# Adding the causal mask on VectorE instead of TensorE, and holding the head norms' small products behind a turning

## The chip, the core and the metric

The kernel runs on one core of a Trainium2 chip. A core has a matrix engine (TensorE, "PE" in the profile, with its weight loads on a row of their own, "PEld"), three engines for elementwise work (VectorE or "DVE", ScalarE or "ACT", GpSimd or "POOL"), and a queue engine (SyncE or "SP"). They run side by side and wait for each other by semaphores. TensorE writes its products to PSUM, eight banks of 128 x 512 float32; VectorE and ScalarE read them there, and all other data lie in SBUF. The metric is the device time of one execution, in microseconds (us).

## What is computed

A decoder trunk of two layers over 512 tokens of width 1024. Layer 0 mixes with attention, layer 1 with a gated short convolution, and each layer ends with a gated MLP. The change touches the attention of layer 0 alone. It has 16 heads of 64 columns: 8 softmax heads with forget gates ("fox") and 8 stick-breaking heads. Queries and keys of every head are normalised first.

```python
q_fox = rms_norm(q[:, :H_FOX], fox_q_g)
k_fox = rms_norm(k[:, :H_FOX], fox_k_g)
...
logits = einsum('bhqd,bhkd->bhqk', qi, k) * scale
logits = logits + fi[..., :, None] - cum_f[:, :, None, :]
causal = key_pos[None, :] <= q_pos[:, None]
logits = jnp.where(causal, logits, -jnp.inf)
p = jax.nn.softmax(logits, axis=-1)
...
# stick-breaking heads
w = jnp.where(strict, jnp.exp(log_beta + later), 0.0)
```

All of it is float32. Queries are handled in blocks of 128; block b sees keys 0 to (b + 1) x 128. Inside the last of these key blocks, the diagonal one, the mask is a triangle.

## The kernel before

**Precision by halves.** A float32 product is made of three products of rounded operands: each operand is split into a high half (`hi`, a rounded copy by ScalarE) and a low half (`lo`, the difference, by VectorE), and hi x hi, hi x lo and lo x hi are summed in PSUM.

**Heads in pairs, blocks in units.** Heads are taken two at a time: pairs p = 0 to 3 are softmax, 4 to 7 are stick-breaking. The query blocks of a pair form three units, `UNITS = (0, 1), (2,), (3,)`: unit 0 holds blocks 0 and 1, units 1 and 2 one block each. So there are 24 units, and the main loop goes through them by number g.

**The steps of a pair.** `queries_keys(p)` (L588) projects keys and queries, 8 steps of three products each (L313 to L315), squares them, and ends with three small groups on TensorE:
- `sums` (L601): sums of squares, 16 narrow products (L607) into a bank "c"; ScalarE copies them (L610);
- `turned_sums` (L613): two transposes (L615) into the same bank, after which VectorE computes the reciprocal roots by a chain of short operations (L617, L399 to L411) and widens them (L633);
- `rows` (L636): four or eight transposes (L640) that spread the roots over a bank "c"; VectorE multiplies (L642), and the result is split into halves (L415 on ScalarE, L416 on VectorE). Softmax pairs spread queries and keys, stick-breaking pairs the keys only.

`logits(p, u)` (L666) makes the scores of one unit: three groups of products of halves (L688), and for softmax heads a fourth with the gate sums. In front of them it calls `need`, which runs fillers until the pair's `rows` have been issued. For softmax heads, 4 products in unit 0 and 2 in the others then add the triangle to the diagonal blocks (L697): an identity in bfloat16 times a 128 x 128 mask of 0 and -1e30. VectorE takes the maximum (L705), ScalarE the exponential with its sum (L706), VectorE the reciprocal and the scaling (L708, L711). For stick-breaking heads ScalarE takes sigmoids (L726, L727), and VectorE scans and multiplies (L729, L732).

`turn(p, b, w)` (L737) transposes the weights of a block for the product with the values: into a bank "c" (L748 for blocks 0 and 1, L760 for 2 and 3, one bank for each of the two heads there), from which ScalarE takes the high half (L754, L763) and VectorE the low half (L755, L764). `weigh(p)` (L767) then multiplies with the values (L784).

**Banks.** PSUM has two banks "a", four "b" (projections and scores) and two "c" (all the small products named above, and the turned weights).

**What sets the order.** The kernel is written as one Python program that keeps a counter of TensorE time, `clock`. `spend(us)` adds an estimate to it, `after(us, fn)` puts a step on a list of due times, and a `spend` that passes a due time runs the step on the spot. `fill(us)` draws "fillers" (steps of the projections, of the values, and of the output projection of the first eight heads) until as much has been spent. In the main loop each g issues the scores of unit g, fills 1.5 (`FILL1`), weighs a pair that is complete, and turns the blocks of unit g - 1, with 3.3 (`FILL2`) of fillers behind each unit's turning. `sums` comes 3.0 after the end of a projection (`SUMS`), `turned_sums` 1.5 after `sums`, `rows` 8.0 after `turned_sums` (`ROWS`). A step of a projection spends 0.65, of the values 0.33, `sums` 0.6, `turned_sums` 0.25, `weigh` 2.4, a turning 0.22 a key block. From the order thus written, a scheduler of the framework sets each engine's queue; it keeps to it except where it expects that an instruction is not ready, and then takes later ones first. On the chip each engine runs its own queue in order.

Of the kernel before, what the change touches and what calls it, by code (L numbers as in the profile page):

```python
# [25 lines left out]
P = 128  # L26
S = 512
NB = S // P
# [14 lines left out]
NORM0 = 4.6  # L43
ORDER = (1, 0, 1, 1, 1, 1, 3)
SUMS, FLAT, ROWS = 3.0, 1.5, 8.0
NSUMS, NROWS, LATE = 4.0, 3.0, 7.0
FILL1, FILL2, BEFORE = 1.5, 3.3, 2.0
UNITS = (0, 1), (2,), (3,)
# [7 lines left out]
def trunk(  # L56
# [167 lines left out]
    def flush():  # L224
        while later:
            later.pop(0)[2]()

    def fill(us):
        quota[0] += us
# [358 lines left out]
    def queries_keys(p):  # L588


        fox = p < 4
        v = tiny.tile([P, 2, NB, 2], F32, tag="qv", name=f"qv{p}")
        r = tiny.tile([P, 2, NB, 2], F32, tag="qr", name=f"qr{p}")
        kept, got, sqs = {}, {}, []
        halves[p] = got

        def pair(i):
            got[i] = [aw.tile([P, S], F32R, tag=f"qk_{n}{i}", name=f"qk_{n}{p}{i}", bufs=2) for n in ("hi", "lo")]
            return got[i]

        def sums():  # L601


            t = bank("c")
            for i in range(2):
                for b in range(NB):
                    pe.matmul(t[32 * b:32 * (b + 1), i * P:(i + 1) * P], head_ones, sqs[i][:, b * P:(b + 1) * P], start=True, stop=True)  # L607
            spend(0.6)
            flat = own.tile([P, S], F32, tag="nrow", name=f"flat{p}", bufs=1)[:, 0:2 * P]
            act.activation(flat, t[:, 0:2 * P], AF.Copy)  # L610
            after(FLAT, lambda: turned_sums(t, flat))

        def turned_sums(t, flat):  # L613
            for i in range(2):
                pe.transpose(t[:, (2 + i) * P:(3 + i) * P], flat[:, i * P:(i + 1) * P], ident)  # L615
            spend(0.25)
            dve.scalar_tensor_tensor(  # L617
                v.rearrange("p i b h -> p (i b) h"), t[:, 2 * P:4 * P].rearrange("p (j c) -> p j c", c=32)[:, :, 0:2],
                1.0 / HD, least[:, :, None].to_broadcast([P, 2 * NB, 2]), op0=ALU.mult, op1=ALU.add,
            )  # L620
            scales()

        def scales():
            vf, rf = (t.rearrange("p i b h -> p (i b h)") for t in (v, r))
            rsqrt(rf, vf, 16, f"qk{p}")
            if not fox:
                s = q_scale[p] = aw.tile([P, 2, NB, 2], F32, tag="qscale", name=f"qscale{p}", bufs=3)
                dve.tensor_copy(s[:, 0], r[:, 1])
                dve.tensor_scalar(s[:, 1], r[:, 1], -1.0, None, op0=ALU.mult)
            wides = {}  # L630
            for i in kept:
                wides[i] = work.tile([P, S], F32, tag="u0", name=f"qwide{p}{i}").rearrange("p (b h d) -> p b h d", b=NB, h=2)
                dve.tensor_copy(wides[i], r[:, i][:, :, :, None].to_broadcast([P, NB, 2, HD]))  # L633
            after(ROWS, lambda: rows(wides))

        def rows(wides):  # L636
            for i in kept:
                t = bank("c")
                for b in range(NB):
                    pe.transpose(t[:, b * P:(b + 1) * P], wides[i][:, b].rearrange("p h d -> p (h d)"), ident)  # L640
                n = work.tile([P, S], F32, tag="y", name=f"qn{p}{i}")
                dve.tensor_tensor(n, kept[i], t, op=ALU.mult)  # L642
                split(*pair(i), n)
            done.add(("qk", p))

        for i in range(2):
            acc = bank("b" if p >= 1 else "a")
            yield from products(acc, weights())
            sq = own.tile([P, S], F32, tag="sq", name=f"sq_{p}{i}")
            act.activation(sq, acc, AF.Square)  # L650
            g = head_gains[:, (0 if fox else 2) + (1 - i):][:, 0:1]
            if i == 1 and not fox:
                hi, lo = pair(i)
                act.activation(hi, acc, AF.Copy, scale=g)
                dve.scalar_tensor_tensor(lo, acc, g, f32(hi), op0=ALU.mult, op1=ALU.subtract)
            else:
                kept[i] = work.tile([P, S], F32, tag="u1", name=f"qk{p}{i}", bufs=3)
                act.activation(kept[i], acc, AF.Copy, scale=g)
            sqs.append(sq)
        after(SUMS, sums)  # L660

    def at_once(u):

# [2 lines left out]
    def logits(p, u):  # L666


        fox = p < 4
        need(("qk", p))  # L670
        need("decay")
        (k_hi, k_lo), (q_hi, q_lo) = (halves[p][i] for i in range(2))
        bs = UNITS[u]
        ss = [bank("b") for _ in range(2)]

        parts, at_ = [], 0
        for i, b in enumerate(bs):
            n = (b + 1) * P
            parts.append((b, n, 256 * i, at_))
            at_ += n  # L680
            spend((4 if fox else 3) * max(n, 256) * 0.00044 + (0.12 if fox else 0))

        def scores(ql, kl, first, last):
            for b, n, c, _ in parts:
                wide = max(n, 256)
                for e in range(2):
                    rows = slice(e * HD, (e + 1) * HD)
                    pe.matmul(ss[e][:, c:c + wide], ql[rows, b * P:n], kl[rows, 0:wide], start=first and b == bs[0], stop=last and b == bs[-1])  # L688

        scores(q_hi, k_hi, True, False)  # L690
        scores(q_hi, k_lo, False, False)
        scores(q_lo, k_hi, False, not fox)
        if fox:
            scores(dl[:, p, :], dr, False, False)
            for e in range(2):
                for b, n, c, _ in parts:
                    pe.matmul(ss[e][:, c + b * P:c + n], ident16, mask, start=False, stop=b == bs[-1])  # L697
        w = aw.tile([P, 2, S], F32, tag="w", name=f"w{p}{u}", bufs=2)
        own = [w[:, :, a:a + n] for b, n, c, a in parts]
        if fox:  # L700
            m = len(bs)
            top, total, inv = (tiny.tile([P, m, 2], F32, tag=f"{t}{m}", name=f"{t}{p}{u}") for t in ("top", "total", "inv"))
            for j, (b, n, c, a) in enumerate(parts):
                for e in range(2):
                    dve.reduce_max(top[:, j, e:e + 1], ss[e][:, c:c + n], axis=AX.X, negate=True)  # L705
                    act.activation(own[j][:, e, :], ss[e][:, c:c + n], AF.Exp, bias=top[:, j, e:e + 1], accum_out=total[:, j, e:e + 1])  # L706
            for es in at_once(u):
                dve.reciprocal(inv[:, :, es], total[:, :, es])  # L708
                for j in range(m):
                    for e in range(es.start, es.stop):  # L710
                        dve.tensor_scalar(own[j][:, e, :], own[j][:, e, :], inv[:, j, e:e + 1], None, op0=ALU.mult)  # L711
        else:

            scale = q_scale[p]
            if not rests:
                rests.append(aw.tile([P, 2, S + 1], F32, tag="rest", name="rest", bufs=1))
                dve.memset(rests[0][:, :, S:S + 1], 0.0)
            rest = rests[0]
            if u == 0:
                dve.memset(rest[:, :, P:P + 1], 0.0)  # L720
            for es in at_once(u):
                for j, (b, n, c, a) in enumerate(parts):
                    end = P if b == 0 else S
                    keys = slice(end - n, end)
                    for e in range(es.start, es.stop):
                        act.activation(rest[:, e, keys], ss[e][:, c:c + n], AF.Sigmoid, scale=scale[:, 1, b, e:e + 1])  # L726
                        act.activation(own[j][:, e, :], ss[e][:, c:c + n], AF.Sigmoid, scale=scale[:, 0, b, e:e + 1])  # L727
                        back = rest[:, e, keys][:, ::-1]
                        dve.tensor_tensor_scan(back, back, begin[:, S - n:S][:, ::-1], 0.0, op0=ALU.mult, op1=ALU.max)  # L729
                for j, (b, n, c, a) in enumerate(parts):  # L730
                    end = P if b == 0 else S
                    dve.tensor_tensor(own[j][:, es], own[j][:, es], rest[:, es, end - n + 1:end + 1], op=ALU.mult)  # L732
        return [(b, x) for (b, n, c, a), x in zip(parts, own)]
# [3 lines left out]
    def turn(p, b, w):  # L737
# [18 lines left out]
        else:  # L756
            for e in range(2):
# [4 lines left out]
                hi, lo = (t_[:, to:to + b + 1, :].rearrange("p k q -> p (k q)") for t_ in pts[p])  # L762
                act.activation(hi, t[:, 0:n], AF.Copy)  # L763
                dve.tensor_tensor(lo, t[:, 0:n], f32(hi), op=ALU.subtract)  # L764
        spend(0.22 * (b + 1))

    def weigh(p):  # L767
# [922 lines left out]
```

## Time and profile before

| | us |
|---|---|
| median of 3 runs (1127.93 to 1128.21) | 1127.98 |
| the profiled execution | 1127.62 |
| its span | 1125.3 |
| TensorE busy | 1115.6 |
| VectorE busy | 943.4 |
| ScalarE busy | 679.9 |

How the lines in the next part are read. A row of a timeline has the start and the length in us, the engine, the line of the kernel, the operation, `out<-in` by the program's names, the shape, a count (like neighbours are merged) and, in brackets, how long the engine was idle before it and what ended that. `psa`, `psb` and `psc` are the banks. A row of the view of waits has the waiting engine and line, whom it waited for, the sum in us, the count and the longest. A row of busy time by stretch has the stretch, its length, and the busy time and count of PE, PEld, DVE, ACT and POOL, then the granted clock of TensorE, the share of the DMA engines and GB/s. A row of a group has the count, the busy time in all and the mean length of one in ns, then the idle time before them and what ended it. TensorE's products overlap, so the length of one is longer than the step from one start to the next.

### The profile page before, as it was taken

How to read it: one execution, taken by the hardware profiler on the slowest of the kernel's cores; microseconds unless marked ns; L12 is line 12 of the kernel's file. 1: busy time of each engine (PE TensorE's matmuls, PEld its weight loads, DVE VectorE, ACT ScalarE, POOL GpSimd, SP SyncE). 2: the span in 40 equal slices, each digit the busy share in tenths (PEclk: the TensorE clock that was granted, in tenths of full speed). 3: DMA queues.
4: the chain of work that ended last, by engine and by line, in shares of the span. 5: the costliest groups of instructions: out<-in, count | busy, mean ns of one | idle time of the engine just before them, and what ended most of it. 6: DMA issues, size and time to landing. Idle time of an engine off the chain costs nothing.

```text
span 1125.3 us, 19407 instructions
## 1 busy us (share of the span) xinstructions
PE 1115.6 (99%) x7691; PEld 1009.8 (90%) x7691; DVE 943.4 (84%) x1439; ACT 679.9 (60%) x1013; POOL 158.6 (14%) x191
## 2 busy tenths in 40 slices
PE   9999999999999999999999999999999999999998
PEld 7888787878899999999999899988889999998886
DVE  6787888887899787888989889875799888898886
ACT  7556676655466766666557455543456766677553
POOL 4011111111101110014400001111111110014300
PEclk9999999999999999999999999999999999999999
DMA  6678777687877777799963455798887766699951
GB/s 194 173 180 200 179 180 200 155 205 206 197 208 201 208 192 197 206 277 205 228 173 77 120 153 125 157 229 216 207 208 188 177 174 159 183 265 195 233 153 57
DMA packets 175690, 209.34 MB, mean 186 GB/s; under 512 B 7564, under 2 KB 140220, under 8 KB 175600
## 3 DMA queue, kind: packets, MB, share of 16 engines
q0 software_dynamic: 41024, 86.95, 39.1%
q1 hardware_dynamic: 134416, 121.09, 34.8%
q8 instruction: 60, 0.98, 0.4%
q14 instruction: 30, 0.25, 0.1%
q10 hardware_dynamic: 160, 0.07, 0.0%
HBM read 203.10 MB, written 49.28 MB: 224 GB/s over the span
## 4 chain that ended last, share of the span: by engine, by line
PE 90%; DVE 4%; issue 2%; DMA 2%; ACT 1%; SPq 0%; DVEq 0%; ACTq 0%; POOLq 0%
PE psb L1056 25%; PE psb L1602 11%; PE psa L1056 10%; PE psa L1602 8%; PE psb L313 5%; PE psb L315 5%; PE psb L314 5%; PE psa L315 3%; PE psa L313 3%; PE psa L314 3%; PE psa L784 2%; PE psb L688 2%; DMA Xc<-in_conv_w_in 2%; PE psb L570 1%; PE psc L315 1%
## 5 line engine op out<-in xcount | busy, mean ns | idle before, releaser
L292 ACT ACTIVATE whi<-raw 128x1024 fp32r<-128x1024 f32 (+2 forms) x89 | 91.7, 1031 | 93.6 <-PE psb L314 29.9
L293 DVE TENSOR_TENSOR wlo<-raw,whi 128x1024 fp32r<-128x1024 f32 (+2 forms) x89 | 105.5, 1185 | 24.2 <-ACT whi L292 23.2
L1056 PE MATMUL psb<-p_lo,whi_p 128*128 128x256 f32 x432 | 121.7, 282 | 0.0
L1056 PE MATMUL psb<-p_hi,wlo_p 128*128 128x256 f32 x432 | 121.6, 281 | 0.0
L1056 PE MATMUL psb<-p_hi,whi_p 128*128 128x256 f32 x432 | 121.4, 281 | 0.0
L313 PE MATMUL psb<-hs_a,whi 128*128 128x512 f32 x224 | 92.2, 412 | 0.0
L315 PE MATMUL psb<-hs_a,wlo 128*128 128x512 f32 x224 | 88.7, 396 | 0.0
L1056 PEld LDWEIGHTS psb<-p_hi,whi_p 128*128 128x128 f32 x432 | 81.9, 190 | 0.0
L1056 PEld LDWEIGHTS psb<-p_lo,whi_p 128*128 128x128 f32 x432 | 81.4, 188 | 0.0
L1056 PE MATMUL psa<-p_hi,wlo_p 128*128 128x256 f32 x288 | 81.2, 282 | 0.0
L1056 PEld LDWEIGHTS psb<-p_hi,wlo_p 128*128 128x128 f32 x432 | 81.2, 188 | 0.0
L1056 PE MATMUL psb<-q_lo,whi_q 128*128 128x256 f32 x288 | 81.1, 282 | 0.0
L1056 PE MATMUL psa<-p_lo,whi_p 128*128 128x256 f32 x288 | 81.1, 282 | 0.0
L1056 PE MATMUL psb<-q_hi,wlo_q 128*128 128x256 f32 x288 | 81.1, 281 | 0.0
L1056 PE MATMUL psa<-p_hi,whi_p 128*128 128x256 f32 x288 | 80.9, 281 | 0.0
L1056 PE MATMUL psb<-q_hi,whi_q 128*128 128x256 f32 x288 | 80.9, 281 | 0.0
L1602 PE MATMUL psb<-act,whi 128*128 128x256 f32 x352 | 63.2, 282 | 0.0
L423 DVE SCALAR_TENSOR_TENSOR uv<-yv,taps,uv 128x511 f32<-128x511 f32 (+1 forms) x80 | 56.6, 744 | 0.0
L1602 PE MATMUL psb<-whi,act 128*128 128x512 f32 x176 | 56.4, 398 | 0.0
L423 DVE SCALAR_TENSOR_TENSOR ug<-yg,taps,ug 128x511 f32<-128x511 f32 (+1 forms) x80 | 55.5, 744 | 0.0
L1056 PEld LDWEIGHTS psa<-p_hi,whi_p 128*128 128x128 f32 x288 | 54.5, 189 | 0.1
L1056 PEld LDWEIGHTS psb<-q_hi,whi_q 128*128 128x128 f32 x288 | 54.6, 189 | 0.0
(478 smaller groups left out, 3619.3 us busy)
## 6 DMA issues: line engine op xcount, KB each, us to landing
t<-in_ffn_w_up POOLq DMA_DIRECT2D x42, 768.0 KB, 8.0
t<-t POOLq DMA_DIRECT2D x18, 768.0 KB, 5.5
raw<-in_attn_w_in SPq DMA_DIRECT2D x24, 512.0 KB, 5.3
X<-in_ffn_w_up SPq DMA_DIRECT2D x18, 512.0 KB, 5.1
Y<-t SPq DMA_DIRECT2D x18, 512.0 KB, 6.6
three<-t SPq DMA_DIRECT2D x18, 512.0 KB, 3.7
W<-in_ffn_w_up SPq DMA_DIRECT2D x18, 512.0 KB, 4.0
X<-in_ffn_w_up POOLq DMA_DIRECT2D x18, 512.0 KB, 8.0
```

The lines of the kernel that those rows point to most:

```text
L292: return (act.activation(hi[:, at_], raw[:, at_], AF.Copy), dve.tensor_tensor(lo[:, at_], raw[:, at_], f32(hi[:, at_]), op=ALU.subtract))
L293: dve.tensor_tensor(lo[:, at_], raw[:, at_], f32(hi[:, at_]), op=ALU.subtract))
L313: made = [pe.matmul(acc, w[0], rhs[0], start=first, stop=False), pe.matmul(acc, w[0], rhs[1], start=False, stop=False), pe.matmul(acc, w[1 ...
L314: pe.matmul(acc, w[0], rhs[1], start=False, stop=False),
L315: pe.matmul(acc, w[1], rhs[0], start=False, stop=last)]
L423: dve.scalar_tensor_tensor(dst[:, d:], src[:, 0:S - d], tap(j), dst[:, d:], op0=ALU.mult, op1=ALU.add)
L570: pe.matmul(acc, lhs[0], w[0], start=first, stop=False)
L688: pe.matmul(ss[e][:, c:c + wide], ql[rows, b * P:n], kl[rows, 0:wide], start=first and b == bs[0], stop=last and b == bs[-1])
L784: pe.matmul(out_, w, t[:, first:first + step * (NB - k - 1) + 1:step, :], start=k == 0 and i == 0, stop=k == NB - 1 and i == 1)
L1056: pe.matmul(to, w[a][:, k, c], x[b][:, k, :], start=fresh and i + k + t == 0, stop=i == 1 and k == 3 and t == 2, skip_group_check=not fresh)
L1602: pe.matmul(to, l, r, start=begin and o + t == 0, stop=end and t == 2 and o == (0 if layer else 1), skip_group_check=not fresh)
```

## The change

1. In `logits`, the mask products of the softmax heads go. The fourth group of scores now ends the accumulation. Instead, before the first maximum of each head of a unit, VectorE adds the mask in place in PSUM, to all diagonal blocks of that head's bank at once: two blocks (columns 0 to 127 and 384 to 511) in unit 0, one in units 1 and 2. The estimate that `logits` spends for a softmax unit keeps its 0.12 a block for the mask.
2. `turn` notes the counter's value at its end and whether the pair is a stick-breaking one. A new function `clear` delays a step until the counter is 2.3 (softmax) or 4.5 (stick-breaking) past that, and looks again then. `sums` and `rows`, when they come due, go through it; `turned_sums` doesn't.

```diff
+CLEAR = 2.3, 4.5
...
+    turned = [-1e9, 0]
+
+    def clear(fn):
+
+        wait = turned[0] + CLEAR[turned[1]] - clock[0]
+        if wait > 0:
+            after(wait, lambda: clear(fn))
+        else:
+            fn()
...
-            after(ROWS, lambda: rows(wides))
+            after(ROWS, lambda: clear(lambda: rows(wides)))
...
-        after(SUMS, sums)
+        after(SUMS, lambda: clear(sums))
...
         if fox:
-            scores(dl[:, p, :], dr, False, False)
-            for e in range(2):
-                for b, n, c, _ in parts:
-                    pe.matmul(ss[e][:, c + b * P:c + n], ident16, mask, start=False, stop=b == bs[-1])
+            scores(dl[:, p, :], dr, False, True)
...
                 for e in range(2):
+                    if j == 0:
+                        diag = ss[e].rearrange("p (k q) -> p k q", q=P)[:, bs[0]:NB:3, :]
+                        dve.tensor_tensor(diag, diag, mask[:, None, :].to_broadcast([P, m, P]), op=ALU.add)
                     dve.reduce_max(top[:, j, e:e + 1], ss[e][:, c:c + n], axis=AX.X, negate=True)
...
+        turned[:] = clock[0] + 0.22 * (b + 1), p >= 4
         spend(0.22 * (b + 1))
```

## The prediction

> **What bounds the kernel now.** I read the page first, then busy time by stretch, then who waited for whom on TensorE, then the timelines around those waits.
>
> ```profile
> span 1125.3 us, 19407 instructions
> PE 1115.6 (99%) x7691; PEld 1009.8 (90%) x7691; DVE 943.4 (84%) x1439; ACT 679.9 (60%) x1013; POOL 158.6 (14%) x191
> ...
> PE 90%; DVE 4%; issue 2%; DMA 2%; ACT 1%; SPq 0%; DVEq 0%; ACTq 0%; POOLq 0%
> ```
>
> TensorE is busy for 99% of the span and holds 90% of the chain that ended last. So an instruction taken from TensorE is worth its own issue time, and a wait of TensorE is worth its length, wherever they lie. The profiled execution took 1127.62 us, 2.3 over its span; the median of the runs is 1127.98, 0.36 more. The sum is made against 1127.62.
>
> The change touches the attention stage only: softmax heads, about 48 to 148 us, then stick-breaking heads to 258 us.
>
> ```profile
> 48.00:148.00 100.00, 99.40 (x711) 81.11 (x709) 80.29 (x213) 62.35 (x141) 12.61 (x17) 1.00 0.77 184
> 148.00:258.00 110.00, 107.41 (x696) 88.50 (x689) 95.13 (x184) 71.11 (x139) 13.24 (x18) 1.00 0.76 189
> ```
>
> The third busy figure is VectorE: 80% in the first stretch, 86% in the second. It has time left in both, but it is a queue that runs in order, so what counts is how late it is when TensorE wants something back.
>
> ```profile
> PE psc L640 <- DVE pt L764: 1.3, 1, 1.3
> PE psc L607 <- DVE pt L764: 1.1, 2, 0.7
> PE psa L784 <- DVE o L791: 0.5, 1, 0.5
> PE psa L784 <- DVE h L830: 0.2, 1, 0.2
> ```
>
> These are all the waits of TensorE from 48 to 258 us that the view names. The two largest rows are the second half of the change: L607 (sums of squares of a head pair) and L640 (its spreading) want one of the two banks "c" that `turn` filled, and VectorE has not yet taken the low half of the turned weights out (L764). The three places are:
>
> ```profile
> 128.51 0.64 PE L607 MATMUL psc<-sq,head_ones 128*32 128x128 f32 x16 [0.44 <-DVE pt L764]
> ...
> 196.38 0.66 PE L640 MATMUL psc<-ident,qwide 128*128 128x128 f32 x4 [1.32 <-DVE pt L764]
> ...
> 205.10 0.65 PE L607 MATMUL psc<-sq,head_ones 128*32 128x128 f32 x16 [0.66 <-DVE pt L764]
> ```
>
> They are the sums of pair 4, the rows of pair 6 and the sums of pair 7: 0.44 + 1.32 + 0.66 = 2.42 us, the first two rows of the waits.
>
> **The mask, TensorE's side.** Per softmax pair 4 + 2 + 2 small products go, 32 in all. The stick-breaking heads run the same scores without a mask, so the trace shows both forms. From the last group of scores to the second product behind it:
>
> ```profile
> 97.44 0.40 PE L688 MATMUL psb<-dr,dl 64*128 64x256 f32 x4
> 97.77 0.40 PE L697 MATMUL psb<-mask,begin 128*128 128x128 bf16 x4
> ...
> 98.29 0.40 PE L314 MATMUL psb<-hs_a,whi 128*128 128x512 f32 x1
> ...
> 104.52 0.33 PE L688 MATMUL psb<-dr,dl 64*128 64x384 f32 x2
> ...
> 105.19 0.39 PE L314 MATMUL psb<-hs_a,whi 128*128 128x512 f32 x1
> ```
>
> ```profile
> 172.80 0.40 PE L688 MATMUL psb<-qk_hi,qk_lo 64*128 64x256 f32 x4
> ...
> 173.47 0.40 PE L314 MATMUL psb<-hs_a,whi 128*128 128x512 f32 x1
> ...
> 179.53 0.34 PE L688 MATMUL psb<-qk_hi,qk_lo 64*128 64x384 f32 x2
> ...
> 180.13 0.39 PE L314 MATMUL psb<-hs_a,whi 128*128 128x512 f32 x1
> ```
>
> With four masks 98.29 - 97.44 = 0.85, without 173.47 - 172.80 = 0.67: 0.18 gained. With two masks 105.19 - 104.52 = 0.67, without 0.60: 0.07. Per pair 0.18 + 0.07 + 0.07 = 0.32, over four pairs **-1.3 us**. The 0.40 us that the view shows for four masks is pipeline depth and would overstate it. The Trainium skill (TensorE: Matmul & The Clock Gate, Back-to-back issue gap) gives about 81 ns for each 128-column product in a stream; by it the 32 would be worth an estimated 2.6 us and the forecast would lie 1.3 lower. The rows go against that: four of them cost 0.18, not 0.32, and the rows decide.
>
> **The mask, VectorE's side.** Added are 24 in-place additions in PSUM, two per unit: 8 over 256 elements (unit 0, both diagonals at once) and 16 over 128. None is in the trace; the nearest rows read PSUM at these sizes.
>
> ```profile
> L705 DVE TENSOR_REDUCE top<-psb 128x1 f32<-128x256 f32 x8 | 3.1, 424 | 1.4 <-ACT w L706 1.4
> ...
> L705 DVE TENSOR_REDUCE top<-psb 128x1 f32<-128x128 f32 x8 | 1.9, 285 | 3.8 <-PE psb L697 3.8
> ...
> L755 DVE TENSOR_TENSOR pt<-psc,pt 128x256 fp32r<-128x256 f32 x4 | 1.7, 422 | 0.1
> ```
>
> The two-operand subtraction of 256 from PSUM (422 ns) equals the reduction (424), so I take 0.42 and 0.285: 8 x 0.42 + 16 x 0.285 = 7.9 us of VectorE within a stretch where it idles for 100 - 80.3 = 19.7. Queued behind each are its `reduce_max`, then ScalarE's exponential, the scaling, and whatever VectorE does next, such as freeing bank "c". So a unit's maximum is late by 0.57 (two of 128) to 0.84 (two of 256), less the 0.07 to 0.18 by which the scores end sooner. The turning of the same weights stands a whole unit later. What hides the additions is VectorE's own idle time: it waited 3.8 us for the scores in unit 0 (row above), and that wait shrinks first. Where that cover is thin:
>
> ```profile
> 66.25 0.67 DVE L642 TENSOR_TENSOR qn<-qk,psc 128x512 f32<-128x512 f32 x1
> ...
> 69.72 1.01 DVE L764 TENSOR_TENSOR pt<-psc,pt 128x384 fp32r<-128x384 f32 x2
> ...
> 119.59 1.02 DVE L764 TENSOR_TENSOR pt<-psc,pt 128x384 fp32r<-128x384 f32 x2
> ```
>
> ```profile
> 66.31 0.55 PE L760 MATMUL psc<-ident,w 128*128 128x128 f32 x3
> ...
> 70.32 0.64 PE L607 MATMUL psc<-sq,head_ones 128*32 128x128 f32 x16
> ...
> 120.20 1.12 PE L640 MATMUL psc<-ident,qwide 128*128 128x128 f32 x8
> ```
>
> Three uses of bank "c" come within some 0.1 us of VectorE's release: the turning at 66.31, just after the L642 before the one shown, the sums of pair 2 at 70.32 and the rows of pair 3 at 120.20, both in the middle of their two L764. The hold does not move these three. Their price lies between nothing (the idle time takes the additions, or other products are ordered ahead) and 3 x 0.57 = 1.7. The turning of six transposes stands in the trace as x3, with other products slipped in, so I stay near the low end: **+0.4**. The Trainium skill (VectorE: DVE Perf Modes, Rules for kernel authors) speaks against this half: count of operations matters on VectorE, since a following one waits for the pipe to empty. The trace agrees only for operations that need each other; by the rule taken whole, 24 more such gaps of an estimated 0.04 us add 1 us to VectorE, which changes no bound here.
>
> **The hold.** I added up the planner's costs for all eight pairs (0.65 a projection step, 0.33 a value step, 0.22 per transposed block, and so on). Since the scores still spend their 0.12 for a mask, nothing moves before the first hold. Five small steps move:
> - sums of pair 4: due at counter 100.54, held by 1.00, run at 101.84, two projection steps later. These are the 0.44.
> - rows of pair 5: due 128.95; each further turning renews the 4.5, so they are released only by the turnings' pause while `need` draws fillers, at 140.39, directly ahead of the scores of pair 5.
> - rows of pair 6: 159.40 to 162.68, again directly ahead of their scores. These are the 1.32.
> - rows of pair 7: 175.60 to 185.07, the same.
> - sums of pair 6: 0.65 later. The sums of pair 7 (the 0.66) are not held, but the fillers drawn earlier bring them from 164.57 to 164.02, ahead of the turning (162.37, now 164.62) that they waited for.
>
> No instruction and no DMA is added or moved with them; fillers drawn up to 3.3 units sooner ask for their weights on SP that much sooner, against two loads of lead. Pair 6's rows show how late VectorE was, and whether 3.28 counter units are enough:
>
> ```profile
> 191.91 1.22 DVE L729 TENSOR_TENSOR_SCAN rest<-rest,begin 128x512 f32<-128x512 f32 x1
> ...
> 193.84 1.22 DVE L729 TENSOR_TENSOR_SCAN rest<-rest,begin 128x512 f32<-128x512 f32 x1
> ...
> 195.77 1.01 DVE L764 TENSOR_TENSOR pt<-psc,pt 128x384 fp32r<-128x384 f32 x2
> ```
>
> The scans stand ahead of L764, which ends its first half at 196.3. TensorE would come over 3 us after 195, so that wait goes. All three go: **-2.4 us**.
>
> What is late next is the scores, which need the rows' products:
>
> ```profile
> 197.07 0.69 DVE L642 TENSOR_TENSOR qn<-qk,psc 128x512 f32<-128x512 f32 x1 [0.28 <-PE psc L640]
> ...
> 198.46 0.69 DVE L416 TENSOR_TENSOR qk_lo<-qn,qk_hi 128x512 fp32r<-128x512 f32 x1 [0.70 <-ACT qk_hi L415]
> ```
>
> ```profile
> 198.58 0.50 PE L688 MATMUL psb<-qk_hi,qk_hi 64*128 64x256 f32 x4
> ...
> 199.33 0.50 PE L688 MATMUL psb<-qk_lo,qk_hi 64*128 64x256 f32 x4
> ```
>
> From rows (196.38) to the scores with the low half (199.33) are 2.95 us with VectorE idle and waiting. In the trace other products were ordered into that time. Now pairs 5, 6 and 7 all go this way, and pairs 5 and 7 meet a busier VectorE. Cover behind each: about 1.3 counter units of fillers, a turning of 0.9, and more fillers, so over 2.95. Low bound: nothing. High bound: each of three chains finds one scan and its multiplication ahead, 195.77 - 193.84 = 1.9, uncovered: 5.8. I take **+0.6**, nearer the low end, since pair 6 in the row shows no wait at its scores.
>
> Sum: -1.3 + 0.4 - 2.4 + 0.6 = -2.7. 1127.62 - 2.7 = 1124.9 for a profiled execution, 1125.3 at the median. That is 0.24%; some 0.2% (2.3 us) is what a measurement of this kernel can tell from no change.
>
> **The rivals.**
> - *The waits only change place.* Bank "c" stays two deep and VectorE as late; the turning ahead of which pair 7's sums now stand, and the scores behind the rows, inherit the 2.4. For it: VectorE is 86% busy there. Against it: TensorE has fillers left for the whole stretch. -1.3 + 0.4: 1127.1.
> - *Rows too close to their scores (slower).* The place is L688 of pairs 5, 6 and 7; the price is the 1.9 of a scan and product ahead of L642, three times, 5.8. It decides from the point where L642 starts more than about 1 us after its transposes. -1.3 - 2.4 + 0.4 + 5.8 = +2.5: 1130.5. For it: the scans and L764 above ran without a gap. Against it: the fillers named.
> - *VectorE becomes the bound in the softmax heads.* All 7.9 us return as waits on bank "c": 7.9 - 1.3 - 2.4 + 0.6 = +4.8: 1132.8. Against it: the 19.7 of idle time.
> - *The hold does not do what it says.* With 4.5 and turnings closer than that, it is `need` that places the rows. That is so by the counter; it is a rival in time only through the second one, and has no chance of its own.
>
> **How the numbers follow.** Forecast 0.58 (its own range 1123.2 to 1126.8, all bounds of the two returns at their low ends giving 1124.3, and about a microsecond for other orders), waits change place 0.21, rows too close 0.14, VectorE bound 0.07. The range 1123.2 to 1130.5 leaves out the last case, half of the second rival and a little of the forecast. Faster by over 0.2% (under 1125.7): most of the forecast, 0.50. Within 0.2%: the rest of it, the first rival and some of the second, 0.30. Slower: 0.20.
>
> **What would show it.** Right: L697 gone, the waits of L607 and L640 on L764 gone, L640 of pairs 5 to 7 right ahead of L688, 24 additions of about 0.28 and 0.42 us. Wrong: a wait of L688 for L416 or L415 over 0.5 us, new waits of L760 or L640 for VectorE between 60 and 125 us, additions over 0.6 us, or TensorE idling for more than 1 us in all in 48 to 258.

## The result, and the profile after

The changed kernel takes 1124.8 us at the median (8 runs, 1123.89 to 1125.72), the kernel before 1128.04 (8 runs beside them). The ratio is 0.9967 with a 95% interval of 0.9958 to 0.9975: 0.33% faster, with 1 outside the interval. The profiled execution took 1125.48 us, 2.14 less than that of before; its span is 2.0 shorter.

The page of the changed kernel, its span and the busy time of each engine:

```profile
span 1123.3 us, 19372 instructions
PE 1114.4 (99%) x7659; PEld 1010.4 (90%) x7659; DVE 947.9 (84%) x1463; ACT 679.8 (61%) x1013; POOL 158.5 (14%) x191
```

VectorE has 24 instructions and 4.5 us more, TensorE 32 products fewer. All lines of the attention behind `clear` stand 11 lower (L688 is now L699, L640 L651, L607 L618, L760 L771, L764 L775), behind the additions 12 (L784 is L796, L791 L803, L830 L842); L313 is now L324. Busy time by stretch, columns as before:

```profile
48.00:148.00 100.00, 99.40 (x687) 80.71 (x687) 85.57 (x238) 62.96 (x142) 12.33 (x17) 1.00 0.77 183
148.00:258.00 110.00, 108.01 (x691) 89.55 (x688) 93.92 (x183) 70.76 (x137) 12.52 (x17) 1.00 0.78 191
```

In the softmax stretch VectorE goes from 80.29 to 85.57 us of 100. All waits that the view of waits names for TensorE from 48 to 258 us:

```profile
PE psa L324 <- DVE rest L731: 1.1, 1, 1.1
PE psa L796 <- DVE h L842: 0.9, 1, 0.9
PE psb L699 <- ACT w L717: 0.6, 1, 0.6
```

The two rows at bank "c" are gone. Of the two at the values (L784, now L796) one is left, with 0.9 in place of 0.2 and 0.5. Two rows are new: one at a bank "a" (the output projection, L324) and one at a bank "b" (the scores, L699). The three places that the hold was to clear, in TensorE's timeline:

```profile
129.76 0.64 PE L618 MATMUL psc<-sq,head_ones 128*32 128x128 f32 x16
...
198.20 0.60 PE L651 MATMUL psc<-ident,qwide 128*128 128x128 f32 x4
199.44 0.64 PE L618 MATMUL psc<-sq,head_ones 128*32 128x128 f32 x16
200.02 0.65 PE L771 MATMUL psc<-ident,w 128*128 128x128 f32 x4
...
201.48 0.51 PE L699 MATMUL psb<-qk_lo,qk_hi 64*128 64x256 f32 x4
```

No row has a bracket: the sums of pair 4, the rows of pair 6 and the sums of pair 7 start without a wait. The sums of pair 7 (199.44) now stand ahead of a turning (200.02), and from the rows of pair 6 to the scores with the low half are 201.48 - 198.20 = 3.28 us without one.

**Where the time went.** Spans differ by things that have nothing to do with the attention, so I measure the attention alone, on TensorE, from one projection product to the first product of the output projection into a bank "c". Before:

```profile
35.91 0.48 PE L313 MATMUL psb<-hs_a,whi 128*128 128x512 f32 x1
...
263.34 0.39 PE L313 MATMUL psc<-o_hi,whi 128*128 128x512 f32 x1
```

After, the same two:

```profile
36.30 0.48 PE L324 MATMUL psb<-hs_a,whi 128*128 128x512 f32 x1
...
262.03 0.39 PE L324 MATMUL psc<-o_hi,whi 128*128 128x512 f32 x1
```

227.43 us before, 225.73 after: **-1.70**. The terms of it that rows show: the mask products -1.3 and the three waits -2.4; the new waits 0.55 at the scores, 1.07 at the output projection, and at the values 0.92 in place of 0.45 + 0.16. That makes -1.3 - 2.42 + 0.55 + 1.07 + 0.31 = -1.8. That this comes so near to -1.70 is in part luck: two amounts of about half a us, which no wait names, nearly cancel (a cost of the additions, below, and a gain that comes with the hold, at e2). The medians differ by 3.2; what of the other 1.5 the change has any part in is taken up below.

The wait at the scores is in the first pair, where ScalarE needs a new table for its first exponential. Its timeline, before and then after:

```profile
51.78 1.28 ACT L706 ACT_TABLE_LOAD   x1
53.08 0.37 ACT L706 ACTIVATE w<-psb,top 128x128 f32<-128x128 f32 x1
```

```profile
53.91 1.28 ACT L717 ACT_TABLE_LOAD   x1 [1.76 <-DVE top L716]
55.21 0.37 ACT L717 ACTIVATE w<-psb,top 128x128 f32<-128x128 f32 x1
```

Before, the load of 1.28 us was done while the scores were still being made. Now it comes behind the first maximum, so the first exponential starts 2.13 us later in the trace (0.39 of it from before the attention, see the first products above), and the second head's scores of unit 1, which want a bank "b" that unit 0 holds, wait (TensorE's timeline of the changed kernel):

```profile
52.45 0.40 PE L699 MATMUL psb<-dr,dl 64*128 64x256 f32 x4
...
53.12 0.40 PE L325 MATMUL psb<-hs_a,whi 128*128 128x512 f32 x1
...
54.59 0.44 PE L699 MATMUL psb<-qk_hi,qk_hi 64*128 64x384 f32 x1
...
55.49 0.50 PE L324 MATMUL psb<-hs_a,whi 128*128 128x512 f32 x1
...
56.77 0.44 PE L699 MATMUL psb<-qk_hi,qk_hi 64*128 64x384 f32 x1 [0.55 <-ACT w L717]
...
57.67 0.50 PE L326 MATMUL psb<-hs_a,wlo 128*128 128x512 f32 x1
...
130.33 0.45 PE L699 MATMUL psb<-qk_hi,qk_hi 64*128 64x384 f32 x2
...
131.23 0.51 PE L324 MATMUL psb<-hs_a,whi 128*128 128x512 f32 x1
```

The first two rows also show the mask's own gain: 53.12 - 52.45 = 0.67 from the last group of scores to the second product behind it, where four masks made it 0.85.

The other rows show a cost of the additions that is no wait. Each of the two heads of unit 1 has four score products. In the first pair the first head's stand alone (54.59 to 55.49, 0.90 us), and the second head's come behind two projection products (56.77 to 57.67, again 0.90). In the last softmax pair the eight products of both heads stand together and take 0.90 in all (130.33 to 131.23). So in the first pair the second head is paid for once more; what that costs against a kernel without additions is read from e5.

The waits at banks "a" come from an order that the hold has shifted. To run the rows of pairs 5 to 7 later, `need` draws fillers in their place, and the fillers left by then are the output projection. It starts at 216.22 us after, at 220.28 before, and its third output wants the first one's bank "a" back at a time when VectorE is busy (timelines of TensorE and of VectorE, changed kernel):

```profile
216.22 0.50 PE L324 MATMUL psa<-o_hi,whi 128*128 128x512 f32 x1
...
223.79 0.47 PE L324 MATMUL psa<-o_hi,whi 128*128 128x512 f32 x1 [1.07 <-DVE rest L731]
...
238.19 1.47 PE L796 MATMUL psa<-pt,v 128*128 128x512 f32 x8 [0.92 <-DVE h L842]
```

```profile
218.59 2.34 DVE L740 TENSOR_TENSOR_SCAN rest<-rest,begin 128x512 f32<-128x512 f32 x2
220.84 1.27 DVE L743 TENSOR_TENSOR w<-w,rest 128x512 f32<-128x512 f32 x2
222.03 1.02 DVE L775 TENSOR_TENSOR pt<-psc,pt 128x384 fp32r<-128x384 f32 x2
222.96 1.30 DVE L842 TENSOR_TENSOR h<-psa,h 128x512 f32<-128x512 f32 x2
223.60 0.06 DVE L731 MEMSET rest<- 128x2 f32 x1
```

The bank is free when the residual addition (L842) has taken it, and the additions stand behind two scans, two products and two low halves, from 218.59 to 222.96 without a gap. The releaser that the view names, a memset of 0.06 us (L731), has nothing to do with a bank; VectorE ran it right behind the first of the two additions, and I read the wait as one for that addition.

### The profile page after: what moved, and what is told of

The parts are those of the page before. It is cut to its first block, busy times and chain, and to the rows that moved or that the text cites. A ratio compares the mean times of both kernels' runs of the same rounds, so it can differ in the third digit from the quotient of the medians.

```text
span 1123.3 us, 19372 instructions
## 1 busy us (share of the span) xinstructions
PE 1114.4 (99%) x7659; PEld 1010.4 (90%) x7659; DVE 947.9 (84%) x1463; ACT 679.8 (61%) x1013; POOL 158.5 (14%) x191
## 4 chain that ended last, share of the span: by engine, by line
PE 96%; DVE 3%; ACT 1%; issue 1%; DVEq 0%; ACTq 0%
PE psb L1068 28%; PE psa L1068 11%; PE psb L1614 11%; PE psa L1614 8%; PE psb L324 6%; PE psb L326 6%; PE psb L325 6%; PE psa L326 2%; PE psa L324 2%; PE psa L325 2%; PE psb L699 2%; PE psa L796 1%; PE psc L771 1%; PE psc L326 1%; PE psc L325 1%; PE psc L324 1%
## 5 line engine op out<-in xcount | busy, mean ns | idle before, releaser
L324 PE MATMUL psb<-hs_a,whi 128*128 128x512 f32 x224 | 92.3, 412 | 0.0
L102 POOL DMA_DIRECT2D t<-in_ffn_w_up x30 | 27.0, 901 | 197.9 <-DMA t<-in_ffn_w_up 106.1
```

Of the source, the lines that this page charges most:

```text
L102: pin(nc.gpsimd.dma_start(to, src[rows, :], accum_op=ALU.add))
L324: made = [pe.matmul(acc, w[0], rhs[0], start=first, stop=False), pe.matmul(acc, w[0], rhs[1], start=False, stop=False), pe.matmul(acc, w[1 ...
```

## The experiments

Medians, ratios to the kernel before run beside each, and the attention's time against the 227.43 of before, measured between the same two products in each profile:

| kernel | median us | ratio, 95% interval | attention |
|---|---|---|---|
| changed | 1124.8 | 0.9967, 0.9958 to 0.9975 | -1.70 |
| changed, again (e8) | 1125.18 | 0.9971, 0.996 to 0.9982 | -1.75 |
| before, again (e9) | 1128.17 | 1.0, 0.999 to 1.0009 | +0.12 |
| e1: additions, no hold | 1125.9 | 0.9981, 0.9972 to 0.9989 | -0.61 |
| e2: hold, mask on TensorE | 1125.45 | 0.998, 0.9971 to 0.9989 | -1.47 |
| e3: held once | 1124.65 | 0.9967, 0.9954 to 0.9979 | -1.80 |
| e4: every addition twice | 1126.8 | 0.9985, 0.9976 to 0.9993 | -1.10 |
| e5: no hold, no mask | 1125.35 | 0.9977, 0.9967 to 0.9986 | -1.74 |
| e6: table loaded early | 1124.23 | 0.9962, 0.9948 to 0.9977 | -2.28 |
| e7: hold 3.4 for 4.5 | 1128.39 | 1.0001, 0.9992 to 1.001 | +2.13 |
| e10: e6 and a bank "b" | 1123.79 | 0.9961, 0.9948 to 0.9974 | -3.14 |
| e11: no hold for softmax heads | 1125.08 | 0.9975, 0.9964 to 0.9985 | -1.54 |

Two profiles of the kernel before differ by 0.12 in the last column, two of the changed kernel by 0.05, so a few tenths can be read there, while the medians carry about a microsecond of uncertainty each.

### e1 and e2: each half of the change alone

e1 keeps the additions and drops the hold:

```diff
-            after(ROWS, lambda: clear(lambda: rows(wides)))
+            after(ROWS, lambda: rows(wides))
...
-        after(SUMS, lambda: clear(sums))
+        after(SUMS, sums)
```

> The additions on VectorE alone, nothing held. Theory (two parts that add): 32 mask products are worth -1.3 us, of which a wait for a bank of the scores behind the first unit takes back about 0.5, so 0.9990 to 0.9995 of before, and the three waits of the sums and rows on the low half of the turned weights stay (about 2.4 us or more, since VectorE is later). Rival (the gain is the mask's): 0.9965 to 0.998. Rival (VectorE's 8 us come back): over 1.001.

e2 keeps the hold and has the mask products back:

```diff
-            scores(dl[:, p, :], dr, False, True)
+            scores(dl[:, p, :], dr, False, False)
+            for e in range(2):
+                for b, n, c, _ in parts:
+                    pe.matmul(ss[e][:, c + b * P:c + n], ident16, mask, start=False, stop=b == bs[-1])
...
-                    if j == 0:
-                        diag = ss[e].rearrange("p (k q) -> p k q", q=P)[:, bs[0]:NB:3, :]
-                        dve.tensor_tensor(diag, diag, mask[:, None, :].to_broadcast([P, m, P]), op=ALU.add)
```

> The mask stays on TensorE, sums and rows are held. Theory: the three waits go (-2.4), and the two new waits on banks a around 222 and 237 us (1.1 and about 0.3 more than before) stay as in the changed kernel, so about -1.0 to -2.0 us, 0.998 to 0.999. Rival (the gain is the mask's): 0.9995 to 1.0005.

The views of TensorE's waits from 48 to 258 us, of e1 and then of e2:

```profile
PE psc L651 <- DVE pt L775: 1.3, 1, 1.3
PE psc L618 <- DVE pt L775: 0.7, 1, 0.7
PE psb L699 <- ACT w L717: 0.5, 1, 0.5
...
```

```profile
PE psa L324 <- DVE rest L731: 1.1, 1, 1.1
PE psa L796 <- DVE h L842: 0.9, 1, 0.9
```

The new waits part cleanly. The one at the scores belongs to the additions (in e1, not in e2), the two at banks "a" to the hold (in e2; in e1 the values wait as before). The hold alone removes all three waits at bank "c". But in e1 the one at the sums of pair 4 (0.44) has gone without a hold. It is gone in e5 too, which has neither hold nor additions, so what removes it there is that the mask products have left TensorE's order. The two halves thus claim the same 0.44, and with the mask products gone the hold removes 1.3 + 0.7.

e1's waits are those that its theory named, but its time is not: the ratio of 0.9981 lies below the 0.9990 to 0.9995 expected, and its interval reaches the range of the first rival. In the attention it gains 0.61, near the 0.8 of the theory; the rest lies behind the attention (see e8 and e9). e2 came within its range. By its waits it should gain 2.42 - 1.07 - 0.31 = 1.04 in the attention and it gains 1.47: some 0.4 us of the hold's gain is in no wait that the view names, and where it lies isn't shown.

### e5: the additions' price

e5 is e1 without the `if j == 0:` block; it leaves the mask out altogether.

> Nothing held, and the mask is left out altogether (softmax heads see the whole diagonal block): TensorE's side of the change alone. Theory (first set of additions is mostly hidden): no wait of the scores for ScalarE around 56 us, and 0.997 to 0.9985, that is 0.3 to 1.0 us below the kernel with the additions alone. Rival (each set of 24 additions costs what the second set cost, about 2 us): 0.9955 to 0.9968.

Its view of waits lacks the row of the scores (L699) and has those of pairs 6 and 7 unchanged. Its attention is 1.74 shorter than before; with 0.44 for the sums of pair 4, which don't wait here either, 1.3 is left for the 32 products, the predicted term. Against e1 the additions cost 1.74 - 0.61 = 1.13 of attention time, of which the named wait is some 0.5. Most of the rest is the parting of the two heads: e1 issues them apart like the changed kernel, while in e5 they are interleaved in part and take 1.33 us (54.52 to 55.85 in TensorE's timeline) where apart they take 0.90 + 0.90, so 0.47 more. Why the order set ahead of the run parts them when the additions are there was not tested. The medians (1125.35 and 1125.9) don't separate the two kernels.

### e4: the additions twice

```diff
                         dve.tensor_tensor(diag, diag, mask[:, None, :].to_broadcast([P, m, P]), op=ALU.add)
+                        dve.tensor_tensor(diag, diag, mask[:, None, :].to_broadcast([P, m, P]), op=ALU.add)
```

> As the changed kernel with every mask addition made twice (the second adds another -1e30 where the mask is, no other value changes). 24 more additions, 7.9 us of VectorE. Theory (VectorE's idle time hides most of them): +0.3 to +1.2 us against the changed kernel, 0.997 to 0.998 of before. Rival (VectorE sets the pace of the softmax heads): +4 to +8 us, over 1.000.

The median is 2.0 above the changed kernel's, the attention 0.6 longer. By either figure a further 7 to 8 us of VectorE cost much less than themselves, and at the median more than the theory allowed (the ratio of 0.9985 lies above its 0.997 to 0.998, and the attention alone within its +0.3 to +1.2). The softmax stretch in e4 (VectorE had 85.57 in the changed kernel):

```profile
48.00:148.00 100.00, 99.59 (x680) 80.77 (x679) 89.23 (x262) 62.62 (x141) 12.48 (x17) 1.00 0.78 190
```

VectorE still idles for 10.8 of 100 us. The view of waits shows no new row (the one at the scores is even down to 0.3), so where the other 1.4 of the median lie isn't settled. It did not become the bound.

### e6: the table loaded early

The changed kernel, and in `decay`, behind the split of the gate sums, one exponential of one column whose result nobody reads:

```diff
+        act.activation(tiny.tile([P, 1], F32, tag="warm", name="table", bufs=1), cum[:, 0:1], AF.Exp)
```

> The changed kernel with one small exponential on ScalarE some 6 us ahead of the first maximum, so that the table for exponentials is loaded before it is wanted. Theory (the 0.55 us wait of the second scores comes from the table load, 1.28 us, that now stands behind the first maximum): the wait goes, 0.4 to 0.6 us below the changed kernel. Rival (the wait comes from the additions): the wait stays at 0.4 or more.

ScalarE's timeline of e6:

```profile
45.64 1.28 ACT L550 ACT_TABLE_LOAD   x1
...
54.09 0.37 ACT L718 ACTIVATE w<-psb,top 128x128 f32<-128x128 f32 x1 [1.77 <-DVE top L717]
```

The exponential now follows the maximum at once, the wait at the scores is gone from the view, and the attention gains 2.28 - 1.70 = 0.58, the wait's 0.55. So that wait was the table's place, not VectorE's load. The two heads of unit 1 still run apart in e6 (from 54.76 and from 56.32 us), so this part of the additions' price stays. At the median (1124.23) the gain can't be told from none.

### e3, e11 and e7: how the hold works

e3 holds a step once and doesn't look again:

```diff
-            after(wait, lambda: clear(fn))
+            after(wait, fn)
```

> As the changed kernel, but a held step isn't held again by a later turning. By the counter the rows of pair 5 then come at 133.88 instead of 140.39 and those of pairs 6 and 7 1.3 and 0.65 sooner than in the changed kernel, still behind a drawn filler; the sums of pair 7 go to 169.36, behind the turning. Theory: the renewal as such isn't needed: within 0.1% of the changed kernel, 0.996 to 0.9975, and the waits for a bank a around 222 us of the same order. Rival (the renewal is what clears the waits): the rows of pair 5 wait on the turned weights, over 0.5 us, 0.998.

e11 holds the stick-breaking heads only:

```diff
-CLEAR = 2.3, 4.5
+CLEAR = -1.0e3, 4.5
```

> The changed kernel without the hold behind softmax turnings (2.3); the 4.5 stays. By the counter the sums of pair 4 come at 100.54 again, the rows of pairs 6 and 7 at 161.36 and 184.42, those of pair 5 at 128.95. Theory (the wait of the sums of pair 4 was gone with the additions alone, so 2.3 does next to nothing): within 0.1% of the changed kernel, no wait of L618 over 0.3 us before 140 us. Rival (the 2.3 pays 0.5 us): L618 waits 0.4 us or more near 128 us.

Both keep the gain, as expected. In both the wait at the values near 237 us is gone and the one at the output projection is 1.5 for 1.1; the attention is 0.1 shorter in e3, 0.16 longer in e11. So looking again pays nothing that can be measured, and the softmax half of the hold (2.3) little or nothing: the only wait it was to remove is the 0.44 that goes when the mask products leave TensorE.

e7 shortens the hold of the stick-breaking heads:

```diff
-CLEAR = 2.3, 4.5
+CLEAR = 2.3, 3.4
```

> The hold behind stick-breaking turnings 3.4 instead of 4.5. By the counter the rows come at 135.18, 160.70 and 177.91 (pairs 5, 6, 7) instead of 140.39, 162.68 and 185.07; only pair 6 is still drawn by its scores, and the output projection isn't drawn ahead. Theory: the wait for a bank a around 222 us (1.1) goes, the rows of pair 6 wait 0 to 0.5: 0.5 to 1.2 us below the changed kernel. Rival (4.5 is needed): the waits on the low half of the turned weights come back, 0.7 us or more above it.

Here the theory missed: the whole gain is lost, 3.6 us at the median (3.2 against the changed kernel's runs in e8). The wait at the output projection did go. The rival's time came, but not by its path: no wait on the low half of the turned weights is back. Waits, then TensorE's and VectorE's timelines of e7:

```profile
PE psc L771 <- DVE qn L653: 3.6, 3, 2.1
...
```

```profile
222.30 0.86 PE L771 MATMUL psc<-ident,w 128*128 128x128 f32 x3 [2.12 <-DVE qn L653]
...
223.38 0.63 PE L325 MATMUL psa<-o_lo,whi 128*128 128x512 f32 x1
223.81 0.63 PE L326 MATMUL psa<-o_hi,wlo 128*128 128x512 f32 x1
```

```profile
218.52 1.22 DVE L740 TENSOR_TENSOR_SCAN rest<-rest,begin 128x512 f32<-128x512 f32 x1
...
220.45 1.22 DVE L740 TENSOR_TENSOR_SCAN rest<-rest,begin 128x512 f32<-128x512 f32 x1
221.58 0.66 DVE L653 TENSOR_TENSOR qn<-qk,psc 128x512 f32<-128x512 f32 x1
```

By the counter, 3.4 releases the rows of pair 5 at 135.18, at the very value at which a turning comes, and those of pair 7 at 177.91, 0.65 ahead of one. Then the rows hold a bank "c" that the turning (L771) wants, and they give it back only when their multiplication (L653) has come through VectorE behind two scans. It is the same bank and the same busy queue as before, with the two sides exchanged: now the turning waits for the rows. With 4.5 the rows go directly ahead of their scores, by the hold at least 4.5 counter units behind the last turning, and some two ahead of the next (pair 6: 162.68 and 164.62). In e3 the rows of pair 5 come 1.30 ahead of a turning (133.88 and 135.18), and none waits. The hold is worth its gain by where it puts the rows, not by its length. Not all that e7 loses is waits, though: about 1.4 us of it go at a lower clock behind the wait of 2.12 (last section).

### e8 and e9: the two kernels once more

> The changed kernel once more, on the same chip as these three: 0.996 to 0.9975, and the same waits (L699 near 56 us, L324 near 222, L796 near 237).

> The kernel before, once more as a kernel of its own, with a profile: 0.9995 to 1.0005. The waits up to 258 us stand as in the first profile (L640 1.3, L607 0.7 and 0.4). What it is to tell: whether the MLP behind the attention, where the change has no instruction, takes the same time in two executions of one kernel. If it does not, a single pair of profiles can't show a gain under about 1 us there.

Both came as expected and repeat their waits and, within 0.12, their attention. The rest of the gain lies behind 264 us, where the change has no instruction, and two differences show there. First, in the convolution of layer 1. TensorE's wait there in the second profile of before (a view of waits, 690 to 720 us):

```profile
PE psb L1056 <- ACT Xsc L1108: 0.7, 1, 0.7
```

TensorE is busy for 35.94 and 35.29 of the 36 us from 684 to 720 in the two profiles of before, for 36.00 in both of the changed kernel. In e9 ScalarE, which makes TensorE's operands, waits there for up to 4.8 us on weights (`Xc<-in_conv_w_in`) that a DMA brings, in the changed kernel for 3.0. Second, in the MLP of layer 0 the products step faster in some executions. Busy time from 324 to 480 us, changed kernel in its first profile and then in e8:

```profile
324.00:480.00 156.00, 156.00 (x1315) 155.99 (x1314) 131.15 (x164) 104.49 (x136) 17.77 (x15) 1.00 0.76 197
```

```profile
324.00:480.00 156.00, 156.00 (x1320) 155.99 (x1320) 131.71 (x165) 105.03 (x137) 17.77 (x15) 1.00 0.75 198
```

1315 products against 1320 in the same 156 us, TensorE busy throughout at a granted clock of 1.00: 156 / 1315 = 118.6 ns and 156 / 1320 = 118.2 ns each, which is 0.6 us in this stretch alone. One kernel shows both, so this difference belongs to the execution and not to the change.

Taken over all runs, though, the gain behind the attention hardly looks like chance. From the product at which the attention's time in the table ends to the end of the span, the two profiles of before take 862.0 and 862.7 us, and the eleven others, whose kernels all have at least a part of the change, 860.1 to 861.6. At the median, too, each of them gains more than its attention does, by 0.3 us (e4) to 2.2 (e7), and e9 doesn't. e7 is the plainest: its attention is 2.13 longer than before and its median the same. So 1.5 of the 3.2 us at the median lie behind the attention, and this speaks for the change having a part in them. By what path isn't shown; the times at which transfers start are one that was not tested.

### e10: the version that combines

e6, and every second output of the output projection into a bank "b":

```diff
-            acc = bank("a")
+            acc = bank("ab"[o % 2])
```

> As the early table load on the changed kernel, and the output projection of the first eight heads takes its banks from a and b in turn. Theory (the waits near 222 and 237 us are this projection and the weighing, held up because VectorE's residual additions stand behind scans): both waits, 1.1 and 0.9, go or fall below 0.3 each, 1.0 to 2.0 us below the early table load alone, 0.9945 to 0.9955. Rival (the scores then wait for a bank b instead): waits of L700 of about 1 us, no gain.

The waits of e10 from 48 to 258 us:

```profile
PE psa L797 <- DVE h L843: 0.8, 1, 0.8
PE psb L700 <- ACT qk_hi L426: 0.4, 1, 0.4
```

The wait at the output projection is gone, that at the values stays, and the scores of pair 7 now wait 0.4 for the high half of their keys. So the theory held for one of its two waits, and the ratio of 0.9961 misses its 0.9945 to 0.9955; in the attention e10 gains 0.86 over e6. The attention is 3.14 shorter than before, 1.44 more than the change brings. Its median of 1123.79 is the lowest of all kernels here, but its interval overlaps the changed kernel's; on the medians alone it isn't shown to be faster.

## Why the prediction was right, step by step

The time forecast was 1125.3, measured 1124.8; the direction and the likeliest case were right. The sum for the attention was -2.7, measured -1.7 to -1.8: the two gains had their sizes, the two returns were twice as large as forecast and stood elsewhere, and about a microsecond and a half of gain behind the attention was in no term. That the median came so near is luck: the attention gave 1.0 less than forecast and what lies behind it 1.5 more.

- **Mask products, -1.3:** held. The step behind the scores is 0.67 as in the unmasked form, and e5 gives 1.3.
- **Additions on VectorE:** lengths held (0.426 and 0.293 us in groups of 8 and 16, forecast 0.42 and 0.285). The groups of the changed kernel:

```profile
L715 DVE TENSOR_TENSOR psb<-psb,mask 128x128 f32<-128x128 f32 x16 | 4.0, 293 | 1.6 <-PE psb L699 1.6
L715 DVE TENSOR_TENSOR psb<-psb,mask 128x256 f32<-128x256 f32 x8 | 3.0, 426 | 2.1 <-PE psb L699 2.0
```

- **Their return, +0.4:** 0.55 is the named wait, and 0.47 more is the second head of unit 1 issued apart; e1 against e5 has 1.13 in all, inside the bounds of 0 and 1.7. The place was wrong. The step named three uses of bank "c" at 66, 70 and 120 us, and none of them waits. What the working missed is the first exponential: I read its table load at 51.78 as done in idle time, and didn't ask whether it would stay ahead of a maximum that became later.
- **Hold, -2.4:** all three waits went, by the shifts that the counter gave: the sums of pair 7 passed a turning, the rows of pair 6 stand ahead of their scores. But 0.44 of it isn't the hold's: it goes with the mask products (e1, e5, e11).
- **The rows' own return, +0.6:** the scores of pairs 5 to 7 wait for no rows, so the price at the place I named is nothing. Instead 1.07 + 0.31 came at banks "a". The step counted what the drawn fillers cover and that their weights load earlier, but not that they are the output projection, which needs a bank back from VectorE in the middle of the scans. This is the step that failed: a filler drawn earlier was taken as free.
- **Rivals.** "The waits only change place" was partly so: of 3.7 us gained in the attention, about 1.9 came back at other banks. VectorE did not become the bound, even with its additions doubled (e4). "Rows too close" did not happen with 4.5, but e7 is its mechanism with another waiter: rows whose multiplication stands behind a scan, 3.6 us of waits, at the turning instead of the scores.
- **Signs.** "TensorE idling for more than 1 us" in 48 to 258 came (1.07 + 0.92 + 0.55 = 2.5), and rightly pointed at returns larger than those of the sum.

## What to carry to other kernels

A small step that waits for a shared buffer is best moved to where neither its predecessor nor its successor on that buffer is near: here a hold shorter by one unit (e7) exchanged the two sides of the wait and, with the clock behind it, lost all of the gain. When a step is held back, look up which work is drawn into its place and what that work needs back, bank by bank, from the engine that was late in the first place. And when an operation is put ahead of an engine's first use of a function, see where the load of its table will then stand.

## What the runs showed of the hardware

- **A stall of some 2 us, and half the clock behind it.** In e7 TensorE's wait of 2.12 us was followed by a stretch at reduced clock. Busy time by stretch of e7, granted clock in the column behind POOL:

```profile
219.00:222.00 3.00, 1.18 (x7) 0.71 (x5) 2.90 (x4) 2.28 (x5) 0.76 (x2) 1.00 0.61 168
222.00:225.60 3.60, 3.30 (x10) 2.72 (x11) 3.60 (x7) 1.12 (x2) 0.00 (x0) 0.55 1.05 193
```

Granted 0.55 in the stretch of 3.6 us behind the wait; the products of 512 columns step by 0.43 us (223.38 to 223.81) where 0.23 is usual. At 0.55 the 3.22 us from 222.30 to 225.52 do the work of 1.8, so some 1.4 us are lost on top of the wait. It is no single event: nine of the eleven runs of e7 show a mean granted clock of 0.998, and the two at 1.0 took 1127.8 and 1126.84 us, less than the others. The single waits of 1.32 us in the kernel before, 1.07 in the changed one and 1.5 in e3 had no such effect: there the profiles grant 1.00. The Trainium skill (TensorE: Matmul & The Clock Gate, Part 1: The HAM clock gate) puts the step to half clock after an idle window of about 3.4 us; in e7 TensorE was idle for 2.12 us, and busy for 1.18 of the 3.00 us from 219 to 222, so an idle time well under that was enough in this one kernel.
- **ScalarE's table load can stand on either side of a wait.** The same load of 1.28 us ran ahead of the maximum at 51.78 us in one kernel and behind it at 53.91 in the other, with only VectorE's work between them changed.
- **Two heads' scores for the price of one.** The score products use 64 rows each ("64*128" in the rows). Four of one head alone took 0.90 us (54.59 to 55.49), eight of two heads side by side 0.90 as well (130.33 to 131.23).
